# Strided columns straight into the compression, zero-padded operands on all 128 rows, and head halves issued in pairs: a two-block model on one NeuronCore

## The chip, the cores and the metric

The program runs on one core of one Trainium2 chip. The metric is the device time of one execution, in microseconds (us). Before the change it is 1012.83 us, the median of 3 runs (1009.8 to 1014.47).

The engines are called as in the profile: PE is TensorE's matmul, PEld its weight load, DVE is VectorE, ACT ScalarE, POOL GpSimd, SP SyncE (which issues the DMAs).

## The reference

Two blocks of two layers each run over 256 tokens of width 1024, in fp32. The first has layer A (a short convolution and latent attention), an MLP, layer C and an MLP. The second has layer AB (sparse attention with a top-k selection, and gated linear attention) and layer CD (retention, and stick-breaking attention). Layer C is where most of the change lies. It has three branches for each of 16 heads in 4 groups: attention to compressed blocks, to selected blocks and to a window. The compression takes 15 blocks of 32 tokens, 16 apart, from keys and values:

```python
n_cmp = (s - CMP_LEN) // CMP_STRIDE + 1          # 15 blocks
starts = np.arange(n_cmp) * CMP_STRIDE           # every 16 tokens
idx = starts[:, None] + np.arange(CMP_LEN)[None, :]

def compress(z, pe, w1, w2):
    blk = z[:, idx] + pe[:, None, :]             # position bias, 32 x 64
    hdn = jax.nn.gelu(jnp.einsum('bnlgd,lde->bnge', blk, w1))
    return hdn @ w2

kc = compress(k_c, pe_k, w1_k, w2_k)
vc = compress(v_c, pe_v, w1_v, w2_v)
...
sc = jnp.einsum('bqgrd,bngd->bgrqn', q_blk, kc).astype(jnp.float32) * scale
...
o_cmp = jnp.einsum('bgrqn,bngd->bqgrd', p_cmp.astype(vc.dtype), vc)
```

In layers AB and CD there are 16 meta tokens ahead of the 256, and their part of the attention runs over 16 keys only.

## The kernel before

**Weights.** All weights are streamed. `Stream.emit` loads a half block of 128 x 1024 (L281), ACT rounds it to fp32r (`hi`, L289) and DVE takes the rest (`lo`, L290), so each half block costs ACT and DVE an instruction of over a microsecond. The large projections are three fp32r matmuls for each product (`mm3`), and every matmul of the kernel goes through `mm` (L328), so rows of L328 are told apart by their tiles. Tile names `xh`, `xl` are the halves of the input, `st` a half block of weights. Matmuls on plain fp32 tiles run as two passes, and the profile counts each.

**Order.** The order on each engine is not written by hand. A scheduler that simulates the engines places the instructions and is free to interleave projections with attention. PSUM has eight banks: two for "d" (projections, tile `pd`), two for "m" (`pm`), four for "w" (`pw`). A bank given out again waits for its last reader.

**Layer C.** `layer_c` first projects the keys and values of the compressed branch (`zs[:2]`) and the keys of the selected and the window branch (`zs[2:]`). `nsa_blocks` scales the former by the row factors into `zz` (64 rows, L1021), copies them shifted by one token to the other 64 rows (L1022, so that a row pair holds two neighbouring tokens), and then makes a second, packed copy: for each of 16 token pairs the 15 blocks of the 4 groups, with the position bias `pe` added (L1027, 16 instructions). `nsa_compress` multiplies these 16 pieces of 60 columns by the weights `w1`, keys on one half of the columns and values on the other, which run together. Gelu and the second weights follow; the compressed keys go to `kbd`, the compressed values to `vbd`, each with 4 heads in blocks of 32 rows.

The keys of both other branches are split in `kcat`'s loop (L926 to L935): `kh` holds the rounded keys on both row halves, `kl` (L934) the rest on one half. `nsa_scores` computes, for each of 8 head pairs, 2 groups and 2 token tiles, `kh` by the query on all 128 rows (its high part on one half, its low part on the other) and then adds `kl` by the high part on 64 rows: 32 times each. `nsa_out` adds the compressed branch (`vbd` by `pct`, 32 rows) and the two others (`pt` by `vt`, half columns) in one bank.

**Layers AB and CD.** `select` and `dsa_scores` multiply queries and keys of one head on 64 of the 128 rows (`akq`), `gla` does so for its scores (`gs`, `kg`) and its state (`gst`); `dsa_out` adds the meta tokens' part (`vb` by `pmt`, 32 rows), `stick_out` likewise (`vb` by `wmt`, 32 rows), and `retention` its own (`am` by `cvt`, 16 rows).

**Normalisation.** Between the layers, `power` sums squares on PE, and DVE and POOL (`rc`, L386 to L389) take the root. PE waits for this at each layer's entry.

## Time and profile before

| | before |
|---|---|
| median of 3 runs, us | 1012.83 (1009.8 to 1014.47) |
| the profiled execution, us | 1015.24 |
| its span, first to last instruction, us | 1013.5 |
| mean granted clock of TensorE | 0.980 |
| PE busy, us | 986.9 (97%) |
| DVE busy, us | 669.7 (66%) |
| ACT busy, us | 517.6 (51%) |
| POOL busy, us | 86.2 (9%) |
| DMA queues | 154.64 MB, mean 153 GB/s |

The profiled execution took 1015.24 us, of which the span from the first to the last instruction is 1013.5. [...] Busy time of PE is modelled: a matmul that waits inside the array for the one before it is busy, so the distance from one start to the next tells more than the mean duration.

### The profile page before, as it was taken

The page shows a single profiled execution, that of the slowest core. Times are in us where ns is not written, and L with a number is a line of the kernel's source. Part 1 is how long each engine was busy: PE and PEld are TensorE (multiplying, and loading weights), DVE is VectorE, ACT ScalarE, POOL GpSimd, SP SyncE. Part 2 cuts the span into 40 slices and gives each one's busy share as a digit, 9 for nine tenths or more (in the row PEclk, how much of TensorE's full clock was granted, in tenths as well). Part 3 has the DMA queues.
Part 4 walks back from the last instruction along what each step waited for, and adds up shares of the span by engine and source line. Part 5 has one row for each costly group of instructions (what it writes and reads, how often), then busy time and mean ns, then how long its engine had stood idle before and what let it go on. Part 6 is the DMA issues. An engine that isn't in the chain of part 4 may idle for free.

```text
span 1013.5 us, 19176 instructions
## 1 busy us (share of the span) xinstructions
PE 986.9 (97%) x7638; PEld 913.8 (90%) x7638; DVE 669.7 (66%) x1372; ACT 517.6 (51%) x933; POOL 86.2 (9%) x112
## 2 busy tenths in 40 slices
PE   7999999999999989999999999999999999999996
PEld 6999989999998967877999999988898679998985
DVE  6889486555555898674855555568977655757752
ACT  6646365444444667564644444455535335454442
POOL 1120010000001000001000000010211201003121
PEclk9999999999999999899899999999999789999999
DMA  9744347555553544211465555547354213643301
GB/s 331 246 163 146 133 139 266 169 193 200 185 172 116 189 156 139 95 58 42 132 235 197 181 175 181 191 143 240 111 172 137 94 43 98 235 129 122 105 1 42
DMA packets 46074, 154.64 MB, mean 153 GB/s; under 512 B 6424, under 2 KB 7968, under 8 KB 45856
## 3 DMA queue, kind: packets, MB, share of 16 engines
q1 hardware_dynamic: 45552, 152.85, 45.1%
q8 instruction: 60, 0.98, 0.4%
q10 hardware_dynamic: 432, 0.57, 0.2%
q14 instruction: 30, 0.25, 0.1%
HBM read 152.33 MB, written 2.70 MB: 153 GB/s over the span
## 4 chain that ended last, share of the span: by engine, by line
PE 94%; DVE 2%; DMA 1%; ACT 1%; issue 1%; POOL 1%; SPq 0%; POOLq 0%; ACTq 0%; DVEq 0%
PE pd L328 46%; PE pw L328 39%; PE pm L328 6%; PE pm L1133 1%; PE pm L1165 1%; DMA x<-in_xT 1%; DMA st<-in_ab_in 1%; POOL rc L389 0%; DVE st L290 0%; PE pm L1506 0%; DVE x L521 0%; PE pm L1704 0%; DVE zz L1027 0%; ACT st L289 0%; PE pw L881 0%
## 5 line engine op out<-in xcount | busy, mean ns | idle before, releaser
L290 DVE TENSOR_TENSOR st<-st,st 128x1024 fp32r<-128x1024 f32 (+2 forms) x274 | 326.6, 1210 | 168.9 <-ACT st L289 168.4
L289 ACT ACTIVATE st<-st 128x1024 fp32r<-128x1024 f32 (+2 forms) x274 | 279.5, 1041 | 276.4 <-PE pd L328 138.8
L328 PE MATMUL pd<-xh,st 128*128 128x256 f32 (+1 forms) x1856 | 360.0, 288 | 8.6 <-ACT st L289 6.3
L328 PEld LDWEIGHTS pd<-xh,st 128*128 128x128 f32 x1856 | 295.4, 191 | 16.7 <-ACT st L289 6.3
L328 PE MATMUL pd<-xl,st 128*128 128x256 f32 (+1 forms) x928 | 265.6, 288 | 0.0
L328 PE MATMUL pw<-hh,st 128*128 128x256 f32 x1024 | 188.4, 283 | 0.0
L328 PEld LDWEIGHTS pd<-xl,st 128*128 128x128 f32 x928 | 177.3, 191 | 2.5 <-issue 1.0
L328 PEld LDWEIGHTS pw<-hh,st 128*128 128x128 f32 x1024 | 161.1, 191 | 0.0
L328 PE MATMUL pw<-hl,st 128*128 128x256 f32 x512 | 144.6, 283 | 0.0
L328 PEld LDWEIGHTS pw<-hl,st 128*128 128x128 f32 x512 | 98.0, 191 | 0.0
L328 PE MATMUL pd<-akq,st 128*128 128x272 f32 (+1 forms) x384 | 78.0, 293 | 0.0
L328 PE MATMUL pw<-xh,st 128*128 128x256 f32 (+1 forms) x384 | 75.1, 285 | 0.8 <-ACT xh L533 0.8
L328 PEld LDWEIGHTS pd<-akq,st 128*128 128x128 f32 x384 | 61.0, 188 | 2.5 <-issue 1.9
L328 PEld LDWEIGHTS pw<-xh,st 128*128 128x128 f32 x384 | 61.2, 189 | 1.4 <-ACT xh L533 1.2
L328 PE MATMUL pd<-gs,st 128*128 128x272 f32 (+1 forms) x192 | 55.3, 288 | 0.0
L328 PE MATMUL pw<-xl,st 128*128 128x256 f32 (+1 forms) x192 | 53.9, 283 | 0.0
L328 PE MATMUL pw<-mh,st 128*128 128x256 f32 x256 | 51.1, 294 | 0.1
L389 POOL TENSOR_TENSOR rc<-rc,mhalf 128x2 f32<-128x2 f32 (+4 forms) x17 | 21.2, 1254 | 323.1 <-DVE rc L386 319.1
L328 PEld LDWEIGHTS pw<-mh,st 128*128 128x128 f32 x256 | 41.8, 197 | 1.3 <-issue 0.6
L487 POOL TENSOR_TENSOR sq<-sq 128x256 f32<-128x256 f32 x12 | 8.9, 740 | 336.1 <-ACT sq L485 335.2
L328 PE MATMUL pw<-ml,st 128*128 128x256 f32 x128 | 37.2, 297 | 0.0
L328 PEld LDWEIGHTS pd<-gs,st 128*128 128x128 f32 x192 | 36.2, 189 | 0.5 <-issue 0.4
(450 smaller groups left out, 1366.8 us busy)
## 6 DMA issues: line engine op xcount, KB each, us to landing
st<-in_w SPq DMA_DIRECT2D x128, 512.0 KB, 4.5
st<-in_ab_in SPq DMA_DIRECT2D x32, 512.0 KB, 3.9
st<-in_cd_in SPq DMA_DIRECT2D x28, 512.0 KB, 4.5
st<-in_a_in SPq DMA_DIRECT2D x18, 512.0 KB, 6.9
st<-in_c_in SPq DMA_DIRECT2D x16, 512.0 KB, 4.6
st<-in_a_out SPq DMA_DIRECT2D x8, 512.0 KB, 5.2
st<-in_c_out SPq DMA_DIRECT2D x8, 512.0 KB, 3.8
st<-in_ab_out SPq DMA_DIRECT2D x8, 512.0 KB, 3.8
```

The lines of the kernel that those rows point to most:

```text
L289: self.last = self.nc.scalar.activation(hi[:, p], raw[:, p], AF.Copy).ins
L290: self.nc.vector.tensor_tensor(lo[:, p], raw[:, p], hi[:, p].bitcast(F32), op=OP.subtract)
L328: self.pe = self.nc.tensor.matmul(out, lhsT, rhs, start=start, stop=stop, skip_group_check=True).ins
L389: nc.gpsimd.tensor_tensor(r, r, self.mhalf[:p, :n], op=OP.pow)
L487: add = lambda e, a, b: e.tensor_tensor(self.sqs[a], self.sqs[a], self.sqs[b], op=OP.add)
L1133: nc.tensor.transpose(tp[:, 128 * j:128 * j + 128], src, self.ident)
L1165: nc.tensor.transpose(ps[:b - a, 128 * j:128 * j + 128], x[:, a:b], self.ident)
```

## The change

**Compression.** The packed copy is left out. The matmuls read every 16th column of `zz` itself (64 bytes apart), 15 blocks from a start that depends on the token pair. `zz` gets a fifth group of 256 columns, zero but for the position bias, which POOL writes (a memset and a small copy for keys and for values). The matmul's output has 75 columns, of which one holds the product of bias and weights, and DVE adds it afterwards as a scalar (`cpe`).

**Full rows.** `kl` becomes as large as `kh`, zero on the other row half (two POOL memsets), and is multiplied on 128 rows. `vbd` gets all 128 rows with zeros outside the head's own (`half` has 8 columns now); so do `vb`, `pmt`, `wmt` and `am`, `cvt` in layers AB and CD, through POOL memsets.

**Joined halves.** In `select`, `gla` and `dsa_scores` the two heads of a row pair are issued one right after the other.

```diff
@@ layer_c
-            kl = lp.tile([128, 2, 512], F32R, name="kl")
+            kl = lp.tile([128, 2, 2, 512], F32R, name="kl")
+            for gg, h in enumerate(HALVES):
+                nc.gpsimd.memset(kl.bitcast(F32)[HALVES[1 - gg], :, gg], 0.0)
...
-                    nc.vector.tensor_tensor(kl[h, gp], k[h], kh[h, gp, gg].bitcast(F32), op=OP.subtract)
+                    nc.vector.tensor_tensor(kl[h, gp, gg], k[h], kh[h, gp, gg].bitcast(F32), op=OP.subtract)
@@ nsa_blocks
-            zz = t[:, :1024].rearrange("p (g n) -> p g n", g=4)
-            b = t[:, 1024:1984].rearrange("p (s g n) -> p s g n", s=16, g=4)
-            zg = zz.rearrange("p (gp gg) n -> p gp gg n", gg=2)
+            zz = t[:, :1280].rearrange("p (g n) -> p g n", g=5)
+            nc.gpsimd.memset(zz[:, 4], 0.0)
+            nc.gpsimd.tensor_copy(zz[:, 4, 0:32:2], cw[:, 16 * a:16 * a + 16])
+            zg = zz[:, 0:4].rearrange("p (gp gg) n -> p gp gg n", gg=2)
...
-            for hf in range(2):
-                for g in range(4):
-                    nc.vector.tensor_tensor(
-                        b[:, 8 * hf:8 * hf + 8, g], zv[:, 0:16:2, g, hf:hf + 15],
-                        pe[:, 8 * hf:8 * hf + 8, None].broadcast_to([128, 8, 15]), op=OP.add)
-            blk.append(b)
+            blk.append(zz.rearrange("p g (n s) -> p s g n", s=16))
@@ nsa_compress
-        hid = ps[:, :60]
+        hid = ps[:, :75].rearrange("p (g n) -> p g n", g=5)
...
-                        blk[a][:, l].rearrange("p g n -> p (g n)"), l == 0, l == 15)
+                        blk[a][:, 2 * (l % 8), :, l // 8:l // 8 + 15], l == 0, l == 15)
...
-        nc.vector.tensor_copy(u, hid)
+        c = lp.tile([128, 1], F32, name="cpe")
+        nc.vector.tensor_copy(c, hid[:, 4, 0:1])
+        nc.vector.tensor_scalar(u.rearrange("p (g n) -> p g n", g=4), hid[:, 0:4], c, None, op0=OP.add)
...
-            for gg in range(2):
-                nc.vector.tensor_scalar(vbd[:, gp, gg], vp, half[:, gg:gg + 1], None, op0=OP.mult)
+            v = self.pair(SEQ, "sq", bufs=4).rearrange("p a (b d) -> p (a b) d", d=64)
+            nc.vector.tensor_tensor(v, vp[:, None, :].broadcast_to([128, 8, 64]),
+                                    half[:, :, None].broadcast_to([128, 8, 64]), op=OP.mult)
+            vbd.append(v)
@@ nsa_scores
-                self.mm(s, q[h], kl[h, gp, :256 * (t + 1)], False, True)
+                self.mm(s, q, kl[:, gp, gg, :256 * (t + 1)], False, True)
@@ nsa_out
-        self.mm(o, vbd[q, gp].rearrange("p g d -> p (g d)"), pct[q, gp].rearrange("p t n -> p (t n)"), True, False)
+        self.mm(o, vbd[gp][:, 2 * r:2 * r + 2].rearrange("p g d -> p (g d)"), pct[:, gp].rearrange("p t n -> p (t n)"),
+                True, False)
@@ gla
-        for hf in range(2):
-            h = 2 * j + hf
-            hs = slice(64 * hf, 64 * hf + 64)
-            p = self.psum("w")
-            for t in range(2):
-                ts = slice(16 + 128 * t, 144 + 128 * t)
-                self.mm(p[:, 128 * t:128 * t + 128], kg[hs, j, ts], qg[hs, j, ts])
-            self.mm(p[0:16, 256:272], kg[hs, j, 0:16], qg[hs, j, 0:16])
+        for t in range(2):
+            ts = slice(16 + 128 * t, 144 + 128 * t)
+            for p, hs in zip(ps, HALVES):
+                self.mm(p[:, 128 * t:128 * t + 128], kg[hs, j, ts], qg[hs, j, ts], t == 0, False)
+        for p, hs in zip(ps, HALVES):
+            self.mm(p[0:16, 256:272], kg[hs, j, 0:16], qg[hs, j, 0:16], False, True)
@@ dsa_meta
-        vb = dp.tile([32, 4, 2, 64], F32, tag="vb", name="vb", bufs=1)
+        vb = dp.tile([128, 4, 2, 64], F32, tag="vb", name="vb", bufs=1)
+        self.pmts = [dp.tile([128, 256], F32, name=f"pmt{i}", bufs=1) for i in range(2)]
+        for v in (vb, *self.pmts):
+            nc.gpsimd.memset(v, 0.0)
@@ dsa_scores
+        ss = [self.psum(bank)[:, :416] for _ in range(2)]
+        for t, c, d in parts:
+            for s, hs in zip(ss, HALVES):
+                self.mm(s[:, c:d], aq[hs, pr, 16 + 128 * t:144 + 128 * t], ak[hs, pr, :d - c], t == 0, t == 1)
@@ layer_cd, stick_out, retention
+            wmt, am = tile([128, 256], "wmt"), tile([128, 2, 256], "am")
+            for v in (vb, wmt, am):
+                nc.gpsimd.memset(v, 0.0)
...
-            self.mm(o, vb[32 * pr:32 * pr + 32, P].rearrange("p a b -> p (a b)"), wm[32 * pr:32 * pr + 32], True, False)
+            self.mm(o, vb[:, P].rearrange("p a b -> p (a b)"), wm, True, False)
...
-                self.mm(o[:, c:c + 128], am[:, f, 128 * t:128 * t + 128], cvt[0:16, 0, vs], c == 0, False)
+                self.mm(o[:, c:c + 128], am[:, f, 128 * t:128 * t + 128], cvt[:, 0, vs], c == 0, False)
```

The change adds no DMA. On PE the number of matmuls stays; only their shapes and their places change. On DVE 16 adds (L1027) are gone. In the rows below a number behind a tile's name tells copies of it apart.

At the entry of the compression DVE has, before the change (`rq` are the scaled row factors, `u` is the compression's output):

```order
L1021 TENSOR_TENSOR zz_4161<-pd,r 64x2x256 x2
L930 TENSOR_TENSOR kcat<-pw,r 128x2x128 x2
L290 TENSOR_TENSOR st_4199<-st_4197,st_4198 128x1024
L290 TENSOR_TENSOR st_4261<-st_4259,st_4260 128x1024
L1027 TENSOR_TENSOR zz_4149<-zz_4149,cw 128x8x15 x8
L930 TENSOR_TENSOR kcat<-pw,r 128x2x128 x2
L1027 TENSOR_TENSOR zz_4161<-zz_4161,cw 128x8x15 x8
L290 TENSOR_TENSOR st_4432<-st_4430,st_4431 128x1024
L290 TENSOR_TENSOR st_4438<-st_4436,st_4437 128x1024
L934 TENSOR_TENSOR kl<-kcat,kh 64x512
L940 TENSOR_TENSOR qt<-pd,rq 128x512
```

and with the change:

```order
L1026 TENSOR_TENSOR zz_4156<-pd,r 64x2x256 x2
L933 TENSOR_TENSOR kcat<-pw,r 128x2x128 x2
L290 TENSOR_TENSOR st_4188<-st_4186,st_4187 128x1024
L290 TENSOR_TENSOR st_4250<-st_4248,st_4249 128x1024
L933 TENSOR_TENSOR kcat<-pw,r 128x2x128 x2
L290 TENSOR_TENSOR st_4423<-st_4421,st_4422 128x1024
L290 TENSOR_TENSOR st_4429<-st_4427,st_4428 128x1024
L937 TENSOR_TENSOR kl<-kcat,kh 64x512 x2
L943 TENSOR_TENSOR qt<-pd,rq 128x512
```

The two rows of L1027 are gone, and `qt` comes behind two pieces of `kl` instead of one.

On POOL, at the entry of layer C (`sq` and `rc` belong to the normalisation ahead of the layer), there stands before the change:

```order
L389 TENSOR_TENSOR rc<-rc,mhalf 128x2
L487 TENSOR_TENSOR sq<-sq 128x256 x3
L1044 MEMSET hd 128x64
L1045 MEMSET kbd 128x64
L389 TENSOR_TENSOR rc<-rc,mhalf 128x2 x2
```

and with it:

```order
L389 TENSOR_TENSOR rc<-rc,mhalf 128x2
L487 TENSOR_TENSOR sq<-sq 128x256 x3
L921 MEMSET kl 64x2x512 x2
L1022 MEMSET zz_4150 128x256
L1022 MEMSET zz_4156 128x256
L1042 MEMSET hd 128x64
L1043 MEMSET kbd 128x64
L389 TENSOR_TENSOR rc<-rc,mhalf 128x2
```

Four memsets stand ahead of the `rc` of the layer's entry.

On PE, in the gated linear attention of the first head pair in layer AB (`kdt` makes the state, `gs,kg` are the scores, `gat` the scores by the values, `gst` the state by the queries, `b` the probabilities to be transposed), there stands before the change:

```order
L328 MATMUL pw<-bvt,kdt 64x128 x4
L328 MATMUL pw<-gs,kg 128x128 x2
L328 MATMUL pw<-gs,kg 16x16
L328 MATMUL pd<-akq 128x144
L328 MATMUL pm<-pmt,vb 128x256
...
L328 MATMUL pd<-akq 128x272
L328 MATMUL pw<-bvt,kdt 64x128 x2
L328 MATMUL pw<-bvt,gat 128x128 x2
L328 MATMUL pw<-bvt,gat 16x128
L328 MATMUL pw<-gst,gs 64x128
L328 MATMUL pw<-gs,kg 128x128 x2
```

and with it:

```order
L328 MATMUL pw<-gs,kg 128x128 x4
L1525 MATMUL pm<-cg,b_9289 128x128
L1525 MATMUL pm<-cg,b_9293 128x128 x2
L1534 MATMUL pm<-cg,pmeta 32x128 x2
L328 MATMUL pw<-gs,kg 16x16 x2
L328 MATMUL pd<-akq 128x144 x2
L328 MATMUL pw<-bvt,kdt 64x128 x2
L328 MATMUL pd<-akq 128x272 x2
...
L328 MATMUL pw<-gst,gs 64x128 x6
L328 MATMUL pd<-xh,st_9179 128x272
L328 MATMUL pd<-xl,st_9179 128x272
```

The scores of both heads stand together, so do the two `akq` of each token tile, and projection matmuls (`xh`, `xl`) follow after 22 rows from the first `kdt`, where before they follow after 38.

## Rows read from the trace of the kernel before

**Rows 1.** The page's head, TensorE's line of the busy times (us, share of the span, instructions), and the shares of the chain that ended last by engine.

```profile
span 1013.5 us, 19176 instructions
PE 986.9 (97%) x7638; PEld 913.8 (90%) x7638; DVE 669.7 (66%) x1372; ACT 517.6 (51%) x933; POOL 86.2 (9%) x112
PE 94%; DVE 2%; DMA 1%; ACT 1%; issue 1%; POOL 1%; SPq 0%; POOLq 0%; ACTq 0%; DVEq 0%
```

**Rows 2.** What PE waited for, over the whole span: us in total, times, longest.

```profile
PE pd L328 <- DVE qt L940: 3.6, 1, 3.6
PE pm L328 <- POOL rc L389: 3.5, 3, 1.2
```

**Rows 3.** The chain that ended last, at the compression: start, us, what.

```profile
354.95 0.75 DVE kcat L930 x2
355.69 2.17 DVE zz L1027 x8
357.87 2.12 DVE st L290 x2
...
360.05 0.68 DVE kl L934
360.73 0.61 DVE qt L940
...
361.39 4.65 PE pd L328 x72
```

**Rows 4.** The instructions of the tile `zz` (the compression's matmuls, the adds), and, of the tile `at`, a VectorE instruction on 128 contiguous elements: count, duration in ns (min/median/max), first and last start, form.

```profile
L328 PE MATMUL pd<-zz,w x64: 222/314/363, 361.4 to 364.7; 128*64 128x60 f32 x64
L1027 DVE TENSOR_TENSOR zz<-zz,cw x16: 348/354/358, 352.8 to 357.5; 128x120 f32<-128x120 f32 x16
...
L1760 DVE TENSOR_TENSOR at<-pw,xl x4: 282/282/282, 958.1 to 969.8; 128x128 f32<-128x128 f32 x4
```

**Rows 5.** Busy time by stretch: stretch, its us, busy us and instructions of PE, PEld, DVE, ACT and POOL, granted clock, DMA share, GB/s.

```profile
346.80:464.00 117.20, 112.88 (x781) 91.09 (x780) 95.64 (x326) 78.42 (x209) 0.00 (x0) 0.96 0.37 123
361.20:364.60 3.40, 3.21 (x60) 3.21 (x62) 3.28 (x6) 2.97 (x5) 0.00 (x0) 0.50 0.61 206
422.60:429.40 6.80, 6.80 (x28) 5.85 (x28) 3.09 (x16) 2.94 (x11) 0.00 (x0) 0.50 0.19 59
798.10:818.60 20.50, 20.50 (x91) 12.21 (x88) 8.16 (x32) 3.62 (x13) 2.41 (x4) 0.50 0.08 27
346.80:381.50 34.70, 31.05 (x243) 26.78 (x242) 32.90 (x92) 23.77 (x50) 0.00 (x0) 0.95 0.52 175
```

**Rows 6.** The timeline of PE in layer C, `kh` and `kl` in turn: start, us from the first start to the last end, line, tiles, rows*columns of the array, form, count.

```profile
420.56 0.38 PE L328 MATMUL pw<-kh,q 128*128 128x256 f32 x1
420.87 0.38 PE L328 MATMUL pw<-kl,q 64*128 64x256 f32 x1
421.18 0.39 PE L328 MATMUL pd<-kh,q 128*128 128x256 f32 x1
```

**Rows 7.** The same view in layer CD: projections, a group of 16-row matmuls, and full-row matmuls of the same number of columns.

```profile
962.00 0.28 PE L328 MATMUL pd<-gs,st 128*128 128x256 f32 x1
962.12 0.28 PE L328 MATMUL pd<-akq,st 128*128 128x256 f32 x1
962.33 0.71 PE L328 MATMUL pw<-cvt,am 16*128 16x128 f32 x4
962.97 0.39 PE L328 MATMUL pd<-akq,st 128*128 128x256 f32 x1
963.19 0.28 PE L328 MATMUL pd<-gs,st 128*128 128x256 f32 x1
...
965.09 1.16 PE L328 MATMUL pw<-cvt,at 128*128 128x128 f32 x8
```

**Rows 8.** The instructions of the tiles `kl`, `pct` and `am` on PE: count, ns, first and last start, forms.

```profile
L328 PE MATMUL pw<-kl,q x20: 379/436/792, 370.2 to 423.4; 64*128 64x256 f32 x10, 64*128 64x512 f32 x10
...
L328 PE MATMUL pd<-kl,q x12: 380/437/506, 421.5 to 455.0; 64*128 64x256 f32 x6, 64*128 64x512 f32 x6
...
L328 PE MATMUL pm<-pct,vbd x16: 374/426/478, 404.1 to 469.5; 32*128 32x256 f32 x16
...
L328 PE MATMUL pw<-cvt,am x16: 270/270/372, 962.3 to 980.7; 16*128 16x128 f32 x16
```

**Rows 9.** The timeline of PE in layer AB, at full clock and, from 804.31, at half clock.

```profile
795.94 0.85 PE L328 MATMUL pw<-gs,kg 64*128 64x128 f32 x6
796.72 0.51 PE L328 MATMUL pd<-akq 64*128 64x144 f32 x2
797.16 0.69 PE L328 MATMUL pm<-pmt,vb 32*128 32x256 f32 x2
797.78 1.31 PE L328 MATMUL pm<-pt,avt 128*64 128x256 f32 x8
...
804.31 1.38 PE L328 MATMUL pw<-gs,kg 64*128 64x128 f32 x6
805.62 0.90 PE L1506 MATMUL pm<-cg,b 128*128 128x128 f32 x3
```

**Rows 10.** The timeline of POOL at layer C's entry, with the idle time before in brackets, and the memset of the tile `qt` at the kernel's start.

```profile
319.57 0.15 POOL L1044 MEMSET hd<- 128x64 f32 x1 [1.17 <-PE pw L328]
319.65 0.15 POOL L1045 MEMSET kbd<- 128x64 f32 x1
321.04 1.66 POOL L389 TENSOR_TENSOR rc<-rc,mhalf 128x2 f32<-128x2 f32 x1 [1.24 <-DVE rc L388]
...
L715 POOL MEMSET qt<- x4: 514/517/519, 0.7 to 2.4; 32x512 f32 x4
```

More of the change, by code (lines that the diff above doesn't have):

```diff
@@ L993, in layer_c, with nsa_gates @@
             self.out_proj(mh, ml, acc)
-    def nsa_gates(self, xh, xl, r, has, gt, lp):
+    def nsa_gates(self, xh, xl, r, has, gt, l2):
         nc = self.nc
@@ L1169, in by_token, with values @@
                 nc.scalar.activation(dst[:b - a, t], ps[:b - a, :128 * n], AF.Copy)
[L1171 removed]
+    def values(self, xh, xl, r, pool, l2, name, zero=False):
         v = pool.tile([128, 3, 512], F32, tag="tok", name=name)
+        if zero:
+            self.nc.gpsimd.memset(v[:, 0], 0.0)
         tmp = []
@@ L1364, in select @@
             for h in range(8):
-                hs = slice(64 * (h % 2), 64 * (h % 2) + 64)
-                p = self.psum("w")[:, :wd]
-                self.mm(p, iq[hs, h // 2, 16 + 128 * t:144 + 128 * t], ik[hs, :wd])
+                if h % 2 == 0:
+                    two = [self.psum("w")[:, :wd] for _ in range(2)]
+                    for p, hs in zip(two, HALVES):
+                        self.mm(p, iq[hs, h // 2, 16 + 128 * t:144 + 128 * t], ik[hs, :wd])
+                p = two[h % 2]
                 rl = l2.tile([128, T2], F32, tag="rl", name="rl")[:, :wd]
@@ L1419, in gla @@
             self.mm(o[0:16, 256:384], at[0:16, 256:272], bvt[0:16, 0, vs], False, False)
-            for c in range(4):
+        for c in range(4):
+            for o, hs in zip(os2, HALVES):
                 self.mm(o[64 * (c % 2):64 * (c % 2) + 64, 128 * (c // 2):128 * (c // 2) + 128],
                         qg[hs, j, 16 + 64 * c:80 + 64 * c], st[hs, c], False, c >= 2)
+        for hf, o in enumerate(os2):
             ob = gp.tile([128, 384], F32, tag="gob", name="gob")
@@ L1489, in dsa_scores @@
             bs = []
-            for t, wd in ((0, 144), (1, 272)):
-                s = self.psum(bank)[:, :wd]
-                self.mm(s, aq[hs, pr, 16 + 128 * t:144 + 128 * t], ak[hs, pr, :wd])
+            for t, c, d in parts:
+                s, wd = ss[g][:, c:d], d - c
                 b = dp.tile([128, wd], F32, tag=f"b{t}", name=f"b{t}")
@@ L1515, in dsa_scores @@
             nc.tensor.transpose(p[0:32, 128 * t:128 * t + 128], pmeta[:, t].rearrange("p a b -> p (a b)"), self.ident)
-        pmt = dp.tile([32, 256], F32, tag="pmt", name="pmt")
-        nc.scalar.activation(pmt, p[0:32, :256], AF.Copy)
+        pmt = self.pmts[pr % 2]
+        nc.scalar.activation(pmt[0:32], p[0:32, :256], AF.Copy)
         return pts, pmt
@@ L1644, in layer_cd @@
             self.mm(p, rep[0:16], dvt[0:16, 0])
-            vb = tile([64, 4, 2, 64], "vb")
-            for g in range(2):
-                nc.vector.tensor_scalar(vb[:, :, g], p.rearrange("p (a b c) -> p a b c", a=4, b=2)[:, :, g],
-                                        half[0:64, g:g + 1], None, op0=OP.mult)
+            vb = tile([128, 4, 2, 64], "vb")
+            wmt, am = tile([128, 256], "wmt"), tile([128, 2, 256], "am")
+            for v in (vb, wmt, am):
+                nc.gpsimd.memset(v, 0.0)
+            nc.vector.tensor_tensor(vb[0:64].rearrange("p (q a) b c -> p q (a b) c", q=2),
+                                    p.rearrange("p (q m c) -> p q m c", q=2, c=64),
+                                    half[0:64, None, :, None].broadcast_to([64, 2, 4, 64]), op=OP.mult)
             stick(1)
@@ L1651, in layer_cd @@
             rotary(ck, rk, slice(0, T2))
-            self.stick_out(0, wts, vb, dvr, mix, l2)
+            self.stick_out(0, wts, vb, dvr, mix, wmt)
             stick(2)
             rotary(cq, r, S)
-            cvt = self.values(xh, xl, r, l2, l2, "cvt")
-            ret = lambda j: self.retention(j, ck, cq, cvt, dect, l2)
+            cvt = self.values(xh, xl, r, l2, l2, "cvt", True)
+            ret = lambda j: self.retention(j, ck, cq, cvt, dect, am, l2)
             stick(3)
@@ L1660, in layer_cd @@
             silu(mix[:, 0:2])
-            self.stick_out(1, wts, vb, dvr, mix, l2)
+            self.stick_out(1, wts, vb, dvr, mix, wmt)
             ret(1)
@@ L1717, in stick_out @@
                                 self.ident)
-        wm = l2.tile([64, 256], F32, tag="wmt", name="wmt")
-        nc.vector.tensor_copy(wm, p[:, :256])
+        nc.vector.tensor_copy(wm[0:64], p[:, :256])
         for pr in range(2):
@@ L1729, in stick_out, with retention @@
             nc.vector.tensor_tensor(mix[:, 4 + P], o, mix[:, 4 + P], op=OP.mult)
-    def retention(self, j, ck, cq, cvt, dect, rp):
+    def retention(self, j, ck, cq, cvt, dect, am, rp):
         nc = self.nc
```

53 lines of the change are left out of this document (26 added, 27 removed).

## The prediction

> **What bounds the kernel.** I read the page first, then TensorE's waits, then the windows of granted clock, then the timeline wherever the change touches something. The page says TensorE: PE is busy 986.9 of 1013.5 us and holds 94% of the chain that ended last [rows 1]. Its waits are few and short, so time comes out of TensorE's own instructions or not at all. Two waits concern this change: 3.6 us for VectorE's `qt`, and 3.5 us in three pieces for GpSimd's `rc` [rows 2]. [...] And "busy" hides something. At full clock 256-column matmuls on all rows start 0.12 us apart (962.00 to 962.12), but the one ahead of four 16-row matmuls takes 0.21 before these begin, the four take 0.64 (eight full-row passes of as many columns start at 965.09 and end 1.16 later, so four are about 0.45 start to start), and the first full-row one behind them takes 0.22 [rows 7]. Each change of the shape of tile thus costs about 0.1 us on the matmul ahead of it and 0.1 on the one behind, within busy time.
>
> **The change part by part.** The profiled execution took 1015.24 us of its own, 2.4 above the median of the three runs (1012.83). I make the sum against 1015.24 and carry the difference over to the median.
>
> *Compression, before the matmuls.* The chain from 354.95 to 361.39 runs over VectorE: `kcat`, eight adds L1027, two weight splits, `kl`, `qt`, and TensorE sits idle 3.6 us for the PSUM bank that `qt` frees [rows 2, 3]. The 16 adds of 354 ns keep VectorE busy for 4.5 us (they overlap: eight take 2.17 in the chain) [rows 3, 4]. Without them `qt` ends near 361.35 − 4.4 = 357.0, just about when TensorE issues its last projection before the gap; the wait goes: −3.6. What is late next is VectorE itself, which was busy 32.9 of 34.7 us around it [rows 5].
>
> *Compression, the matmuls.* 64 passes (32 pairs that run together) took 3.3 us at half clock, right behind the idle time [rows 4, 5]. At full clock, with 75 columns instead of 60, I estimate 3.3 / 2 × 75 / 60 = 2.1: −1.2. No row shows TensorE streaming columns 64 bytes apart. The nearest is the VectorE add that read the same tile with the same step: 354 ns for 120 elements against 282 for a contiguous 128 [rows 4], a factor 1.26, which would be 0.5 us here. I take 0.3: −0.9 net. Bounds: 0 to 5 (four times as long per column). The clock may also stay low for other reasons; then 1.2 is lost.
>
> *The low half of the keys on full rows.* 32 matmuls `kl` on 64 rows stand between `kh` on 128 rows [rows 8]. From 420.56 to 421.18 one `kh` and one `kl` of 256 columns take 0.31 each [rows 6]; on full rows they would take 0.12 each as in [rows 7]. So each `kl` costs 0.38 us in shape changes: 32 × 0.38 = −12.2. Padding adds nothing to the streaming, since the columns stay the same.
>
> *Compressed values, meta, stick.* In the 32-row two-pass matmuls one of two changes goes (the neighbour behind is a half-column tile of another shape): `pmt` takes 0.62 for two passes (797.16 to 797.78) [rows 9]; two 256-column fp32 passes at four 128-column passes in 0.45 are 0.45. That is 0.17 to 0.2 each: 8 × 0.2 = −1.6 for `pct` [rows 8], −0.8 for 4 `pmt`, −0.8 for 4 `wmt`.
>
> *Retention.* Four groups of 16-row matmuls at (0.21 − 0.12) + (0.64 − 0.45) + (0.22 − 0.12) = 0.38 [rows 7, 8]: −1.5. With `wmt` some −2.3; I take −2.0 since one of the shown groups has its later neighbour close by.
>
> *Joined halves.* A visit of `gs,kg` costs 0.78 us (795.94 to 796.72) and a lone 144-column `akq` 0.44 [rows 9]. Two heads on two row halves run together, so two of four `gs,kg` visits go (−1.6), and two pairs of lone `akq` (about −1.0). Against it, in the new order two transposes stand between the `gs,kg` and its 16-row rest, and value tiles and state tiles alternate more, each change 0.1 to 0.2. With the 0.8 of `pmt` I take −2.2 for layer AB.
>
> *Half clock.* 422.6 to 429.4 follows directly upon the alternation of `kh` and `kl`, in which TensorE is "busy" mostly by shape changes; 28 passes took 6.8 us [rows 5], at 0.12 to 0.23 each they would take some 3.8: −3.0 if the clock stays up. 798.1 to 818.6 lies in an unbroken run of small tiles; the same `gs,kg` group takes 0.78 there at full and 1.31 at half clock [rows 9], so 20.5 us hold some 12.5 to 13.5 of work. The new order brings projection matmuls back in the middle of that run, so that it may end earlier, but the small tiles before them stay: −2, bounds 0 to −6.
>
> *GpSimd's queue at layer C's entry.* This is the loss. `rc` at 321.04, on TensorE's path (1.2 us of its wait), now stands behind two memsets of `kl` and two of `zz`, which can start no earlier than `hd` did, at 319.57 [rows 10]. The nearest rows are memsets of 64 columns (152 ns) and 512 (517), so some 0.9 for the 1,024 of each `kl` and 0.3 for the 256 of each `zz`: 319.57 + 2.4 + 0.2 = 322.2 instead of 321.04: +1.1 (bounds 0.5 to 1.8). The other memsets (`vb`, `pmt`, `wmt`, `am`, `cvt`) stand where GpSimd is idle; if not, 0.5 each.
>
> *What VectorE takes back.* From 346.8 to 464 TensorE was busy 112.9 of 117.2 us and VectorE 95.6 [rows 5]. The terms above take 3.6 + 0.9 + 12.2 + 1.6 + 3.0 = 21.3 from TensorE's path: 95.9 would be left. VectorE loses 4.5 and gains a little: 91.3, so it would have to be busy 95%, which is what it reached from 346.8 to 381.5 (32.9 / 34.7) with everything ready for it. At 90% the stretch takes 101.4, a gain of 15.8; at the 82% of before (95.6 / 117.2) 111.9, a gain of 5.3. I take 90%: −16.
>
> Sum: −16 (layer C) + 1.1 (its entry) − 2.2 (AB) − 2 (its clock) − 2 (CD) = −21: 994 for an execution like the profiled one, 992 beside the median.
>
> **Rivals.** *VectorE takes most of it.* Against my 90%: softmax and evictions answer one another through PSUM and never reached that from 405 on, as the whole stretch's 82% shows. Layer C then gains 5 to 9, the rest stays: 1012.8 − 7 − 5 = 1001. For it: VectorE is the only thing left to wait for.
>
> *Everything comes.* VectorE at 95% (−21), the long half-clock stretch mostly gone (−6), AB and CD −4, entry +0.5: 982.
>
> *The strided reading is slow.* If the 64 passes take four times as long per column, compression's matmuls take 8.4 us at full clock instead of 2.1: 6 us more than I count, 998. For it: VectorE's add was 1.26 times as long as a contiguous one [rows 4]; against it: it was far from four times. [...]
>
> [...]
>
> *The change doesn't do what it says.* The extra 0.38 could belong to the order `kh`, `kl` into one bank rather than to the rows used. Then 12.2 + 1.6 + 2.3 stay and only the compression comes: 1012.8 − 5 − 2 + 1 = 1007. Against it: 16-row and 32-row tiles into other banks show the same 0.1 on either side [rows 7, 9].
>
> **How the numbers follow.** My forecast, 985 to 999, 0.62; VectorE takes most, or slow strides (997 to 1004), 0.22; everything comes (980 to 985), 0.09; it doesn't do it, 0.04; slower, 0.03. The likeliest is 992. The range 982 to 1002 leaves 2 in 10 outside. A difference below 0.5% (5 us) can't be told from none in this kernel. Faster: 0.62 + 0.22 + 0.09 + 0.02 = 0.95, of which I keep 0.94; same 0.03; slower 0.03.
>
> **What would show it.** Right: TensorE's wait for `qt` gone and no half clock around the compression; `kh` and `kl` starting 0.12 (256 columns) and 0.23 (512) apart; no half clock near 422; VectorE over 85% busy through layer C, and TensorE's list of waits there headed by VectorE; `rc` at the entry about 1 us later. Wrong: `zz` pairs further apart than 0.07 us; `kl` still 0.3; TensorE's waits in layer C over 12 us; half clock there in long pieces.

## Result and the profile after

The changed kernel took **984.39 us** (median of 4 runs, 983.2 to 984.84) beside 1011.32 us for the kernel before (4 runs, 1006.01 to 1014.47): a ratio of 0.9737, 95% interval 0.9692 to 0.9782. The forecast was 992 us, in a range of 982 to 1002. The direction and the range held; the gain was 27 us where the sum gave 21, and 984.39 lies in the interval that the prediction called "everything comes" (980 to 985, a chance of 0.09), below the 985 to 999 that it called its forecast.

The page of the changed kernel's profile, its head and its busy times (us, share of the span, instructions), beside [rows 1], and what PE waited for, beside [rows 2]:

```profile
span 982.6 us, 19181 instructions
PE 960.6 (98%) x7638; PEld 903.5 (92%) x7638; DVE 664.5 (68%) x1354; ACT 515.6 (52%) x933; POOL 91.0 (9%) x125
```

```profile
PE pd L328 <- ACT st L289: 6.3, 1, 6.3
PE pm L328 <- POOL rc L389: 3.7, 3, 1.4
```

TensorE does the same 7638 passes in 26 us less of busy time. The 6.3 us for `st` are the start of the kernel and stand in the list of the kernel before as well. The 3.6 us for `qt` are gone, the wait for `rc` is nearly as it was (3.7 beside 3.5).

Three stretches tell most. Busy time by stretch in the changed kernel (columns as in [rows 5]): the same work of layer C that took 117.20 us before, the compression's matmuls, and the gated linear attention (`kdt` to the last `gst`):

```profile
346.40:446.50 100.10, 98.67 (x782) 87.72 (x781) 89.00 (x306) 77.52 (x208) 0.00 (x0) 1.00 0.45 144
357.60:362.00 4.40, 4.40 (x66) 4.23 (x64) 3.70 (x5) 4.20 (x6) 0.00 (x0) 1.00 0.29 115
779.70:806.80 27.10, 27.10 (x232) 20.73 (x231) 18.63 (x64) 11.09 (x34) 3.81 (x5) 1.00 0.21 69
```

The last of these took 40.5 us in the kernel before, at a mean granted clock of 0.75 (a share of full speed; 0.50 is called half clock); in the old order 16 more passes of other work lie between its first and last matmul:

```profile
795.20:835.70 40.50, 40.50 (x248) 28.72 (x247) 21.97 (x72) 13.23 (x40) 4.09 (x6) 0.75 0.16 53
```

Layer C gave 17.1 us. VectorE was busy 89.0 of its 100.1 us, and TensorE waited less than 1.5. Most of that is one wait for ScalarE, the longest in TensorE's list for this stretch:

```profile
PE pm L328 <- ACT pt L1142: 1.1, 1, 1.1
```

The stretch of 20.5 us at half clock in layer AB [rows 5] is gone altogether.

The timeline of PE shows the shape changes gone. `kh` and `kl` in turn, now both on 128 rows (start, us to the last end), beside [rows 6]:

```profile
406.80 0.28 PE L328 MATMUL pd<-kh,q 128*128 128x256 f32 x1
406.92 0.28 PE L328 MATMUL pd<-kl,q 128*128 128x256 f32 x1
407.03 0.39 PE L328 MATMUL pw<-kh,q 128*128 128x512 f32 x1
407.27 0.39 PE L328 MATMUL pw<-kl,q 128*128 128x512 f32 x1
407.50 0.28 PE L328 MATMUL pw<-kh,q 128*128 128x256 f32 x1
```

Starts are 0.12 us apart for 256 columns and 0.23 to 0.24 for 512, where `kh` and `kl` of 256 columns took 0.31 each before. In layer CD the four matmuls of `am` and the projection ahead of them, beside [rows 7]:

```profile
932.97 0.28 PE L328 MATMUL pd<-akq,st 128*128 128x256 f32 x1
933.09 0.60 PE L328 MATMUL pw<-cvt,am 128*128 128x128 f32 x4
933.45 0.36 PE L328 MATMUL pd<-akq,st 128*128 128x256 f32 x1
933.66 0.28 PE L328 MATMUL pd<-gs,st 128*128 128x256 f32 x1
```

From 932.97 to 933.66 are 0.69 us; the same six took 1.07 (962.12 to 963.19) before.

**The clock differs from one execution to the next.** Each execution comes with its mean granted clock, and 31 further ones of the kernel before, run beside the experiments, spread over 15 us along it. In the traces of both kernels the clock is 1.00 or 0.50 and nothing between, so the time at half clock is twice what the mean falls short of 1, times the span.

| kernel before, executions | clock | at half clock, us | us |
|---|---|---|---|
| three at 0.993 | 0.993 | 14 | 998.9, 999.4, 1001.1 |
| median of 31 | 0.985 | 30 | 1007.68 |
| slowest | 0.978 | 44.5 | 1014.15 |

A straight line through all 31 rises 0.46 us for each us at half clock. The changed kernel's four executions had 0.992, or 15.7 us at half clock. So at an equal clock the change is worth 15 to 16 us: 999.8, the mean of the three, beside 984.65 in a later execution at 0.993, or 1000.7, where the line stands at 15.7 us, beside 984.4. The rest, 7 to 12 in the medians, is clock that the changed kernel keeps.

Not all of the time at half clock is lost to TensorE. In every kept trace the last 3 to 5.5 us of the span are at half clock, and they lie behind TensorE's last matmul, as in the changed kernel:

```profile
978.20:982.60 4.40, 0.00 (x0) 0.00 (x0) 0.24 (x1) 0.21 (x1) 0.00 (x0) 0.50 0.33 121
```

So an execution with less than 23 us at half clock in all cannot have had the whole stretch of 20.5 us. By that, 7 of the 31 executions of the kernel before (10 to 22 us) did without it, though nothing was changed in them.

### The profile page after: what moved, and what is told of

It reads as the page before. It is cut to its first block, busy times and chain, and to the rows that moved or that the text cites. A ratio compares the mean times of both kernels' runs of the same rounds, so it can differ in the third digit from the quotient of the medians.

```text
span 982.6 us, 19181 instructions
## 1 busy us (share of the span) xinstructions
PE 960.6 (98%) x7638; PEld 903.5 (92%) x7638; DVE 664.5 (68%) x1354; ACT 515.6 (52%) x933; POOL 91.0 (9%) x125
## 4 chain that ended last, share of the span: by engine, by line
PE 95%; DVE 1%; POOL 1%; issue 1%; DMA 1%; ACT 1%; SPq 0%; POOLq 0%; ACTq 0%
PE pd L328 47%; PE pw L328 39%; PE pm L328 6%; PE pm L1137 1%; PE pm L1169 1%; DMA x<-in_xT 1%; POOL rc L389 0%; PE pm L1525 0%; PE pm L1727 0%; DVE pm L1121 0%; DVE x L521 0%; PE pw L881 0%; DVE st L290 0%; PE pw L1652 0%; POOL kl L921 0%
## 5 line engine op out<-in xcount | busy, mean ns | idle before, releaser
L328 PE MATMUL pw<-mh,st 128*128 128x256 f32 x256 | 49.0, 286 | 0.1
L328 PEld LDWEIGHTS pw<-xl,st 128*128 128x128 f32 x192 | 36.4, 190 | 0.0
```

The lines of the kernel that those rows point to most:

```text
L328: self.pe = self.nc.tensor.matmul(out, lhsT, rhs, start=start, stop=stop, skip_group_check=True).ins
```

## Experiments

All are medians of whole executions beside 984.4 of the changed kernel, unless an edit says that it starts from the kernel before. The clock moves these as well: ten executions of the changed kernel took 981.3 and 981.6 us at 0.997 and 983.2 to 985.0 at 0.991 to 0.993. So a difference of 2 us is read beside executions of the same clock, or in the traces.

**Keys' low half on 64 rows again.** From the changed kernel:

```diff
-                self.mm(s, q, kl[:, gp, gg, :256 * (t + 1)], False, True)
+                h = HALVES[gg]
+                self.mm(s, q[h], kl[h, gp, gg, :256 * (t + 1)], False, True)
```

> The changed kernel, with only the low half of the keys multiplied on its own 64 rows again (32 matmuls); the padded tile stays. Shape-change theory: each of the 32 visits costs 0.38 us again, so 984.4 + 12.2 = 996.6, up to 1000 if TensorE also falls to half clock in the alternation of kh and kl. Rival, the time went with VectorE's 16 adds: 984 to 988, since the adds stay away here.

Measured: 995.53 us (4 runs, 991.25 to 996.08). The timeline of PE has the old distances back:

```profile
412.22 0.36 PE L328 MATMUL pw<-kh,q 128*128 128x256 f32 x1
412.51 0.38 PE L328 MATMUL pw<-kl,q 64*128 64x256 f32 x1
412.82 0.39 PE L328 MATMUL pd<-kh,q 128*128 128x256 f32 x1
413.13 0.38 PE L328 MATMUL pd<-kl,q 64*128 64x256 f32 x1
```

0.31 each again, and +11.1 us for 32 of them, or 0.35 us each. At an equal clock it is 10 to 11 (991.25 at 0.998 beside 981.3 and 981.6 at 0.997; 995.32 beside 984.4 at 0.992). The shape-change theory stands, the rival falls: VectorE's adds were still away. Behind this alternation the clock falls, too: from 415.2 to 418.4 it is 0.50 here, in the changed kernel it is 1.00 through the whole stretch of layer C above.

**The packed copy back.** From the changed kernel, with the 16 adds that fill `b` as before, and without `cpe`:

```diff
-            zz = t[:, :1280].rearrange("p (g n) -> p g n", g=5)
+            zz = t[:, :1024].rearrange("p (g n) -> p g n", g=4)
+            b = t[:, 1024:1984].rearrange("p (s g n) -> p s g n", s=16, g=4)
...
-            blk.append(zz.rearrange("p g (n s) -> p s g n", s=16))
...
+            blk.append(b)
...
-                        blk[a][:, 2 * (l % 8), :, l // 8:l // 8 + 15], l == 0, l == 15)
+                        blk[a][:, l].rearrange("p g n -> p (g n)"), l == 0, l == 15)
```

> The changed kernel, with only the packed copy and its 16 adds back (60 contiguous columns). Shape-change theory: the 3.6 us wait for qt comes back, the matmuls get shorter (4.5 us measured with strides; 1.9 at full, 3.3 at half clock): 984.4 + 3.6 - 1.2 to - 2.6 = 985.4 to 986.8. Rival, VectorE was what bound layer C: its 4.5 us come back in full and push evictions back too, 990 or more.

Measured: 984.42 us (4 runs, 982.83 to 986.77), no difference. The timeline of PE at the compression, packed:

```profile
359.26 2.08 PE L328 MATMUL pd<-zz,w 128*64 128x60 f32 x64 [2.14 <-DVE qt L943]
361.27 0.39 PE L328 MATMUL pd<-xh,st 128*128 128x256 f32 x1
```

and of the changed kernel:

```profile
357.72 4.53 PE L328 MATMUL pd<-zz,w 128*64 128x75 f32 x64
362.18 0.39 PE L328 MATMUL pd<-xh,st 128*128 128x256 f32 x1
```

Packed: 2.14 us of waiting and 2.01 of matmuls. Strided: no wait and 4.46 of matmuls. What the change takes off VectorE it puts on TensorE: 2.45 us of matmuls for 2.14 of waiting. The rival that VectorE bounds layer C falls as well, since its 4.5 us are back here and show up nowhere but in those 2.14. Half clock did not come back with the wait in this trace. It is not the wait's length alone that decides: with the compression of the kernel before and joined heads (an experiment below), TensorE waited 2.1 us for `qt`, and the clock was 0.50 from 360.6 to 363.8.

**What a stride costs.** From the changed kernel, to see whether the distance from column to column is the price; the compression reads other columns and so computes something else:

```diff
+        cols = [16] * 4 + [4] * 4 + [2] * 4 + [1] * 4
...
-                        blk[a][:, 2 * (l % 8), :, l // 8:l // 8 + 15], l == 0, l == 15)
+                        blk[a][:, :, 0:15 * cols[l]:cols[l]], l == 0, l == 15)
```

> The changed kernel, with other columns read in the compression's matmuls: 5 x 15 columns as before, but 16 elements apart for the first 4 of the 16 token pairs, 4 apart for the next 4, then 2, then 1. So the compression computes something else; the rest is the same. With strides the changed kernel's pairs started 131 to 143 ns apart. [...] Rival, the short rows of 15 columns or the two row sums cost it: 131 at every step.

The one execution took 981.7 us; since it computes something else, only its rows count here. Busy time of `zz`'s instructions on PE, by stretch; each stretch ends where the next step's first pass starts (the last one with the start of the last pass), and a pass under way counts in both:

```profile
356.13:357.26 1.13, 1.13 (x17) 1.00 0.79 272
357.26:358.36 1.10, 1.10 (x21) 1.00 0.36 145
358.36:358.95 0.59, 0.59 (x20) 1.00 0.04 14
358.95:359.42 0.47, 0.47 (x21) 1.00 0.00 0
```

Eight pairs took 1.13 us at step 16 (64 bytes), 1.10 at step 4 (16 bytes), 0.59 at step 2, and seven and a half 0.47 at step 1: 141, 138, 74 and some 63 ns a pair. So the distance is the price, and the rival falls: the rows of 15 columns and the two row sums are the same at every step. The price is not the 64 bytes, it begins between 8 and 16: 8 bytes cost 74 ns beside 63 for columns side by side, 16 cost 138. Why it begins there no run shows.

The steps come one after another, and the DMA engines grow idle meanwhile (shares of 0.79, 0.36, 0.04 and 0.00 above). That is not the cause: steps 16 and 4 cost the same at 0.79 and 0.36, and the packed columns of the experiment before ran fast at 0.81 (63 ns a pair):

```profile
359.26:361.27 2.01, 2.01 (x64) 1.95 (x64) 1.95 (x4) 1.99 (x4) 0.00 (x0) 1.00 0.81 312
```

**Block order.** From the changed kernel; VectorE writes `zz` so that the 15 columns of a pair lie side by side:

```diff
-            zz = t[:, :1280].rearrange("p (g n) -> p g n", g=5)
+            zz = t[:, :1280].rearrange("p (g s n) -> p g s n", g=5, s=16)
...
-                nc.vector.tensor_tensor(zg[0:64, :, gg, :], z[s], rb[s], op=OP.mult)
-            nc.scalar.activation(zz[64:128, 0:4, 0:255], zz[0:64, 0:4, 1:256], AF.Copy)
-            blk.append(zz.rearrange("p g (n s) -> p s g n", s=16))
+                for gp in range(2):
+                    nc.vector.tensor_tensor(zz[0:64, 2 * gp + gg].rearrange("p s n -> p n s"), ...)
+            nc.scalar.activation(zz[64:128, 0:4, 0:16:2], zz[0:64, 0:4, 1:16:2], AF.Copy)
+            blk.append(zz.rearrange("p g s n -> p s g n"))
```

> The changed kernel, with keys and values written by VectorE in block order (16 token places, then 16 blocks, in each group), so that the compression's matmuls read runs of 15 columns that lie side by side; the shifted copy takes half the elements. If the distance of the columns is the price, the 64 passes take 2.2 to 2.5 us instead of 4.5, and VectorE pays for writing 64 bytes apart: four instructions of 0.69 become eight of 0.35 to 0.7. 982 to 984 beside 984.4. Rival: VectorE's writes cost more than TensorE saves, 984.5 to 986.

Measured: 981.78 us (4 runs, 980.77 to 983.99). The tile `zz` there:

```profile
L328 PE MATMUL pd<-zz,w x64: 228/228/279, 359.6 to 361.7; 128*64 128x75 f32 x64
...
L1026 DVE TENSOR_TENSOR zz<-pd,r x8: 597/610/615, 347.0 to 350.7; 64x256 f32<-64x256 f32 x8
```

The 64 passes take 2.1 us and TensorE waits 0.4 us for `qt`; VectorE's eight writes take 610 ns each for 256 elements, not much less than the 0.69 us for 512 elements in the changed kernel, so it pays about 2 us off TensorE's path. Run once more beside the changed kernel on one chip:

> The changed kernel with keys and values in block order once more: 1.5 to 3 us below the changed kernel on the same chip, since its 64 passes take 2.1 us instead of 4.5 and nothing else on TensorE's path changes; if what was measured came from the clock, the two are within 1 us.

> The changed kernel once more, on one chip with the one in block order, to tell them apart: 984.4 again, clock 0.99, between 983 and 987.

Measured: 982.31 us (6 runs, 982.12 to 983.11) beside 984.51 (6 runs, 981.27 to 984.97). At clocks of 0.991 to 0.993 the changed kernel took 984.4 to 985.0 and the block order 982.1 to 983.1; two executions of the changed kernel at 0.997 were faster than any of these. So the gain of 2 us is of the size expected at like clocks, and smaller than what the clock does between two executions (3.5 us).

**Memsets behind the root.** As the block order, with the memsets of layer C's entry held back:

```diff
-                nc.gpsimd.memset(kl.bitcast(F32)[HALVES[1 - gg], :, gg], 0.0)
+                with tc.issue_after(root):
+                    nc.gpsimd.memset(kl.bitcast(F32)[HALVES[1 - gg], :, gg], 0.0)
...
+            with self.tc.issue_after(root):
+                nc.gpsimd.memset(zz[:, 4], 0.0)
```

> As the one in block order, and the four memsets at layer C's entry are held back until GpSimd has done the root there. If the queue on GpSimd is what delays the entry: rc starts at once behind VectorE's sum, 1.4 us earlier, but if it then takes 1.6 us as in the kernel before instead of 0.7 as in the changed one, only 0.4 us come. So 0.4 to 1.4 us below the one in block order.

Measured: 981.27 us (4 runs, 981.04 to 984.5), not to be told from 981.78. The timeline of POOL in the changed kernel, beside [rows 10]:

```profile
318.93 1.95 POOL L921 MEMSET kl<- 64x1024 f32 x2 [1.21 <-PE pw L328]
...
320.82 0.56 POOL L1022 MEMSET zz<- 128x256 f32 x2
...
321.53 0.70 POOL L389 TENSOR_TENSOR rc<-rc,mhalf 128x2 f32<-128x2 f32 x1
```

and of DVE and POOL with the root first:

```profile
320.94 1.22 DVE L290 TENSOR_TENSOR st<-st,st 128x1024 fp32r<-128x1024 f32 x1
321.07 1.66 POOL L389 TENSOR_TENSOR rc<-rc,mhalf 128x2 f32<-128x2 f32 x1 [1.24 <-DVE rc L388]
```

The queue does delay the root: it starts 2.60 us after POOL comes free (318.93 to 321.53) instead of 1.47 (319.57 to 321.04). But it then takes 0.70 instead of 1.66 us. Where it took 1.66, here and in the kernel before, it ran beside a weight split of VectorE; delayed, it runs when that is over. A third case lies between. In the kernel before with full rows for the keys (an experiment below), the root starts 0.42 us before the split ends and takes 0.99:

```profile
320.72 1.22 DVE L290 TENSOR_TENSOR st<-st,st 128x1024 fp32r<-128x1024 f32 x1
...
321.52 0.99 POOL L389 TENSOR_TENSOR rc<-rc,mhalf 128x2 f32<-128x2 f32 x1
```

In both cases with an overlap the root ends some 0.57 us behind the split (320.94 + 1.22 = 322.16 and 322.73; 321.94 and 322.51), as if it stood still until then. That the split is the reason was not tried apart. For TensorE little is left of the delay. It waits 1.18 us for this root in the kernel before and 1.40 in the changed one:

```profile
322.75 0.71 PE L328 MATMUL pm<-cg,rc 128*128 128x128 f32 x4 [1.18 <-POOL rc L389]
```

```profile
322.28 0.87 PE L328 MATMUL pm<-cg,rc 128*128 128x128 f32 x4 [1.40 <-POOL rc L389]
```

**The two heads one after the other; small operands on their own rows; both.** From the changed kernel, `gla` and the first lines of `dsa_scores` as before:

```diff
-        for t, c, d in parts:
-            for s, hs in zip(ss, HALVES):
-                self.mm(s[:, c:d], aq[hs, pr, 16 + 128 * t:144 + 128 * t], ak[hs, pr, :d - c], t == 0, t == 1)
...
+                self.mm(s, aq[hs, pr, 16 + 128 * t:144 + 128 * t], ak[hs, pr, :wd])
```

> The changed kernel, with the two heads of a row pair issued one after the other again in the gated linear attention and in the sparse attention's scores (not in the selection, where the order on TensorE was the same before). If the new order is what keeps TensorE at full clock there: 2.6 us for the lone matmuls and about 7 for a stretch of some 20 us at half clock, 994. If that stretch is chance: 987. Rival, joining is worth nothing: 984 to 985.

Measured: 985.79 us (4 runs, 985.56 to 986.59, clocks 0.993 to 0.995), so +1.4. The traces give a similar figure: from the first `pmt` to the first `wmt`, all at full clock, it is 136.00 us here (lines below) and 134.95 in the changed kernel (766.32 to 901.27), +1.05. At an equal clock the difference may be larger, since the changed kernel had 984.65 at 0.993 and 981.6 at 0.997. The other, from the changed kernel:

```diff
-        self.mm(o[:, 16:272], vb[:, pr].rearrange("p a b -> p (a b)"), pmt, True, False)
+        self.mm(o[:, 16:272], vb[0:32, pr].rearrange("p a b -> p (a b)"), pmt[0:32], True, False)
...
-                self.mm(o[:, c:c + 128], am[:, f, 128 * t:128 * t + 128], cvt[:, 0, vs], c == 0, False)
+                self.mm(o[:, c:c + 128], am[0:16, f, 128 * t:128 * t + 128], cvt[0:16, 0, vs], c == 0, False)
```

(and likewise `vbd` by `pct` and `vb` by `wmt`, 32 rows each).

> The changed kernel, with the small operands on their own rows again: compressed values by probabilities (32 rows, 8 times), meta tokens (32 rows, 4 times), stick-breaking's meta part (32 rows, 4 times), retention's (16 rows, 16 matmuls in 4 groups); the zero-padded tiles stay. Shape-change theory: 1.6 + 0.8 + 0.8 + 1.5 = 4.7, so 989. Rival, half of these changes stay because a neighbour has another shape anyway: 984.4 + 1.5 (retention alone) = 986.

Measured: 986.49 us (4 runs, 985.99 to 987.64), so +2.1 in the medians, between the two expectations. But the clock was higher here: at 0.997 it took 986.10 and 986.88, where the changed kernel took 981.3 and 981.6; at 0.991 987.64 beside 984.9 and 985.0. So at an equal clock it is 2.7 to 5.6.

The traces show what each of the tiles gave, since the order of TensorE's matmuls around them is the same in both kernels. From the start of the matmul ahead to the start of the one behind, `am` costs 1.5 us more on 16 rows (all four groups), `pct` 1.3 more on 32 rows (seven of eight), `wmt` 0.4 (two of four), `pmt` 0.3 (two of four): 3.5 in all. `pmt` gains 0.19 where a full-row matmul stands ahead. Where a 64-row `akq` does, it takes 0.62 on 32 rows and 0.63 on 128:

```profile
784.09 0.69 PE L328 MATMUL pm<-pmt,vb 32*128 32x256 f32 x2
784.71 0.87 PE L328 MATMUL pm<-pt,avt 128*64 128x256 f32 x8
```

```profile
783.39 0.70 PE L328 MATMUL pm<-pmt,vb 128*128 128x256 f32 x2
784.02 0.87 PE L328 MATMUL pm<-pt,avt 128*64 128x256 f32 x8
```

So the rival of this run is right in part: where the neighbour ahead has another shape anyway, padding gains nothing. Both edits together:

> The changed kernel, with both the heads one after the other and the small operands on their own rows again; layer C's compression and the keys' full rows stay. In layer AB TensorE then has the instructions of the kernel before, in its order, and in the same forms. If each undoing adds its own price: 984.4 + 1.4 + 2.1 = 988. If the half clock of some 20 us in layer AB hangs on the tiles and the order there: granted clock down to 0.98 and a stretch of over 10 us at half clock in most executions, 993 to 997. If that stretch was the kernel before's own bad luck, 988 at a clock of 0.99 or more.

Measured: 996.72 us (6 runs, 990.86 to 997.13), at clocks of 0.986 in four of the six. That is 12.3 more than the changed kernel, where the two alone add up to 3.5 in the medians. Busy time by stretch of the gated linear attention, both heads apart; small operands narrow; and, in two rows, both edits (the whole, and its part at half clock):

```profile
777.40:809.00 31.60, 31.60 (x246) 23.88 (x247) 21.51 (x72) 13.17 (x40) 4.17 (x6) 1.00 0.20 68
```

```profile
780.40:807.50 27.10, 27.10 (x232) 20.71 (x231) 18.62 (x64) 11.08 (x34) 3.81 (x5) 1.00 0.21 67
```

```profile
777.80:818.00 40.20, 40.20 (x243) 28.90 (x242) 21.33 (x69) 12.44 (x40) 4.08 (x6) 0.75 0.16 53
```

```profile
780.70:801.20 20.50, 20.50 (x85) 12.77 (x86) 8.17 (x31) 4.87 (x19) 2.42 (x4) 0.50 0.07 25
```

With both undone the stretch of 20.5 us at half clock is back, at the place where it was before. The first `pmt` and the first `wmt` of both edits, and then of the heads apart alone:

```profile
766.94 0.69 PE L328 MATMUL pm<-pmt,vb 32*128 32x256 f32 x2
912.20 0.69 PE L328 MATMUL pm<-wmt,vb 32*128 32x256 f32 x2
```

```profile
767.45 0.60 PE L328 MATMUL pm<-pmt,vb 128*128 128x256 f32 x2
903.45 0.59 PE L328 MATMUL pm<-wmt,vb 128*128 128x256 f32 x2
```

They lie 145.26 us apart with both edits, 136.00 with the heads apart, 135.20 with small operands (766.74 to 901.94), 134.95 in the changed kernel, and 145.22 in the kernel before (785.13 to 930.35). The shapes and the order are worth 1.05 + 0.25 of this, so the stretch itself costs 145.26 − 134.95 − 1.3 = 9.0.

With the heads apart alone, TensorE has the same instructions in the same order there as in the kernel before but for `vb` by `pmt`, which is on 128 rows instead of 32, and stays at full clock. So the stretch does not hang on the order alone, as the prediction had it; in these runs either edit was enough to be rid of it: all four executions of each had at most 18 us at half clock in all, and so had all ten of the changed kernel. But the old instructions do not bring it every time. With both edits two of the six executions (990.86 and 993.48, clocks of 0.990 and 0.991) have too little time at half clock for it, as have the 7 of 31 of the kernel before. So the edits change how often it comes, from most executions to none that was seen.

**Joined heads in the kernel before.** Only `gla` and `dsa_scores` of the changed kernel, in the kernel before:

```diff
+            for p, hs in zip(ps, HALVES):
+                self.mm(p[:, 128 * t:128 * t + 128], kg[hs, j, ts], qg[hs, j, ts], t == 0, False)
```

> The kernel before, with only the two heads of a row pair issued together in the gated linear attention and in the sparse attention's scores. If the new order there is what keeps the clock up: 1007.7 - 1.4 - 6 to - 8 = 998 to 1000, with no stretch of 20 us at half clock. If the clock there is chance: 1006 and the same spread as the kernel before.

Measured: 1000.71 us (12 runs, 995.56 to 1004.03), 7.1 below the kernel before beside it. Some 5 of these are clock, as was expected: the median execution has 20 us at half clock instead of 30, and ten of the twelve have at most 22. At 0.990 the two kernels are close (999.25 to 1004.03 in five executions beside 1001.1 and 1002.5). The profiled execution has no half clock there (busy time by stretch, 31 us from the first `kdt` on):

```profile
794.00:825.00 31.00, 31.00 (x263) 24.52 (x260) 19.91 (x70) 13.37 (x47) 4.52 (x5) 1.00 0.19 55
```

**Full rows for the keys in the kernel before.** Only `kl`, with its larger tile and memsets as in the change:

```diff
-                self.mm(s, q[h], kl[h, gp, :256 * (t + 1)], False, True)
+                self.mm(s, q, kl[:, gp, gg, :256 * (t + 1)], False, True)
```

> The kernel before, with only the low half of the keys zero-padded and multiplied on all 128 rows. Shape-change theory: 12.2 us less than before at the same granted clock; with the half clock near 422 gone, 15. The stretch at half clock in layer AB stays, since nothing was changed there, if it comes from the order of work there; if it hangs on chance, it may be missing. So 993 to 997 beside 1008. Rival, the adds on VectorE are what bound layer C: 1004 or more.

Measured: 994.93 us (4 runs, 986.93 to 999.86) beside 1007.61. The spread is the clock: 986.93 came at 0.996, 999.86 at 0.981. Executions at an equal clock (0.990, 20 us at half clock: 992.09 here, 1001.1 and 1002.5 of the kernel before) differ by 9 to 10, as the 10 to 11 of the opposite edit. The stretch in layer AB is there in the profiled execution; two of the four (at 0.990 and 0.996) have too little time at half clock for it.

## Why the prediction was right or wrong, point by point

**What bounds the kernel: right.** The time came out of TensorE's own instructions, by the shapes that change between them, and out of its clock.

**The sum against the two profiled executions.** The prediction worked from an execution of 1015.24 us; that of the changed kernel took 984.41, and the spans differ by 30.9.

| term | forecast, us | between the two traces, us |
|---|---|---|
| layer C | −16 | −17.1 |
| its entry | +1.1 | +0.2 |
| layer AB, shapes and order | −2.2 | −1.3 |
| layer AB, half clock | −2 | −9.0 |
| layer CD | −2 | −1.9 |
| sum | −21 | −29.1 |

Of the 8 us between the two sums 7 are the half clock in layer AB.

**Full rows for the keys: right.** 12.2 was forecast; it is 10 to 11 by undoing it, 9 to 10 by doing it alone.

**VectorE taking back part of layer C: right in size, by luck.** The terms added up to 21.3, and a limit of 90% busy on VectorE was to leave 16 of them; it came to 89.0 of 100.1 us and a gain of 17.1. But VectorE was not what limited the stretch: TensorE waited less than 1.5 us there, mostly for ScalarE, and the packed copy brings VectorE's 4.5 us back for 2.14 us of waiting. The sign named for it, a list of TensorE's waits headed by VectorE, did not come. What was missing from the 21.3 was mostly the compression's matmuls, next the keys, which gave 1 to 2 less than forecast.

**The compression: wrong.** The wait for `qt` went as forecast, and with it the half clock around it. But the term "strided matmuls", estimated at 2.1 and set at 2.4, measured 4.5, and the sign of being wrong that was named for it (pairs further apart than 0.07 us) came true at 0.14. The 0.3 for the stride rested on a VectorE add, and the factor of 1.26 read off it compares 120 elements with 128; for each element it is 1.34, which is still too little. Together with 2.1 us of waiting instead of 3.6 in the packed version of the changed kernel, the whole part is worth 0.0 instead of 4.5. The rival named for it, that the strided reading is slow, was right, at about twice the price per column (141 ns a pair beside some 63) instead of four times.

**The small operands: right for `am` and `pct`, half for the others.** The working had 1.6 (`pct`), 0.8 (`pmt`), 0.8 (`wmt`) and 1.5 (`am`), 4.7 in all. The traces show 1.3, 0.3, 0.4 and 1.5, or 3.5. The step that was too large is that a change of shape goes at every visit: ahead of half of the `pmt` and `wmt` stands a tile of another shape. The 2.1 of the medians is too low, since the clock was higher in that run.

**Joined heads: right.** Without `pmt` the working had 2.2 − 0.8 = 1.4; it is 1.4 in the medians and 1.05 in the trace. Two heads on two row halves do run together: the four `akq` passes of 144 columns of both take 0.45 us in the changed kernel (781.92 to 782.37), the two of one head 0.44 in the kernel before (796.72 to 797.16).

**GpSimd's queue: the start was right, the cost wrong.** The root's start came 1.13 us later, as forecast (1.1), but the root became 0.96 shorter, so TensorE's wait for it grew by 0.2 only.

**Half clock: mis-sized, and this is most of the difference.** −3 for 422 and −2 for layer AB were in the sum. The former is inside layer C's 17.1, and undoing the full rows brings half clock back at its place. The latter measured −9.0, since the stretch disappeared as a whole instead of ending early. The step that failed is "the small tiles before them stay": the clock did not fall at all, and the reason given (projections back in the middle of the run) is not the only one, since with the old order and `pmt` on full rows it does not fall either. The rival "everything comes" had this stretch mostly gone, at −6. There is luck in this term on the other side, too: the execution that the prediction worked from had the stretch, and about one in four of the kernel before does not.

Undone one by one, the parts give 11.1 + 0.0 + 1.4 + 2.1 = 14.6 in the medians, and 16.0 with the 3.5 of the traces for the small operands; the difference at an equal clock is 15 to 16. The clock adds the other 7 to 12 in the medians.

## What to carry to other kernels

Where TensorE is busy all the time, look at the distances of the starts at every change of tile shape: here some 0.2 us for a single visit to another shape (`pct`, `pmt`, `wmt`), 0.35 where shapes alternate (`kl`), were bought off by zero padding, which cost a memset and no streaming (`kl` of 256 columns takes 0.12 us from start to start on 128 rows, 0.31 on 64). It paid where the neighbours are on full rows; behind a tile of yet another shape it gave nothing (0.62 us on 32 rows, 0.63 on 128). Look at the distance of the columns that TensorE reads as well: in fp32 a pair of passes took 74 ns at 8 bytes and 138 at 16. If a copy is there anyway, let it write them in the order in which they are read (2.1 us instead of 4.46 for the 64 passes). And before a gain is divided among the parts of a change, compare executions at the same granted clock, or add up distances in the traces: the medians put the small operands at 2.1 us, where the traces have 3.5. A stretch at half clock worth 9 us came in most executions with two small parts undone together and in none with only one of them undone, so undoing the parts one at a time does not show it.

## What the runs showed that was not expected

- A matmul pass on two column halves, 75 columns in fp32: 141 ns a pair at 64 bytes from column to column, 138 at 16, 74 at 8, some 63 at 4.
- GpSimd's root of 128 x 2 elements: 1.66 us where it starts with a weight split on VectorE, 0.99 where it starts 0.42 us before the split ends, 0.70 without one.
- The same instructions in the same order, four passes of them on 128 rows instead of 32, and TensorE's granted clock stays at 1.00 instead of falling to 0.50 for 20.5 us. On 32 rows it falls in most executions and not in all (four of six with both edits). What exactly tips it is open.
